# Two and six PSUM banks in place of three and five, in a kernel of two transformer layers

## The chip, the cores and the metric

The kernel runs on one core of one Trainium2 chip. The metric is the device time of one launch in microseconds (us); lower is better. The engines have these names in the profile: PE is TensorE (matmuls), PEld the loading of its weights, DVE is VectorE, ACT is ScalarE, POOL is GpSimd, SP issues most of the transfers (DMA).

## The reference, cut to what matters

Two layers run one after the other on 256 tokens (T) of width 2048, all in fp32. What matters here is that nearly all the work is products of the activations with big weight matrices, with smaller work between them:

```
proj = x @ w_in + b_in                        # layer 1, 42 column tiles of 128 here
y_conv = silu(layer_norm(conv31(c_val * sigmoid(c_glu)))) * silu(c_gate)
y_attn = window_attention_with_sinks(q, k, v) * silu(a_gate)
x = layer_norm(alpha * x + concat(y_conv, y_attn) @ w_out + b_out)
h = rms_norm(x)                               # layer 2
... = split(h @ w_in_2)                       # sparse attention (NSA), gated linear attention (GLA)
x = x + concat(o_nsa, o_gla) @ w_out_2
x = x + cross_attention(rms_norm(x), rms_norm(mem)) @ w_co
x = x + (silu(gg) * uu) @ w_down              # gg, uu = split(rms_norm(x) @ w_gu)
```

## The kernel before

**Products.** A weight matrix is read in pieces of 128 x 1024 fp32 numbers. `fetch` loads a piece into a ring of four buffers (`st`, L309), ACT rounds it to `hi` (L312) and DVE takes the rest `lo = st - hi` (L313); `hi` and `lo` have rings of four too. Three products of hi and lo parts stand for one fp32 product. `fm2` (through `mm2`, L350 and L352) makes one output tile of 128 columns from two pieces: sixteen matmuls of 512 columns with the hi weights (against hi and lo activations side by side) and sixteen of 256 columns with the lo weights, all summed in one PSUM bank. `tm` (with `mm3`, L325 to L327) makes tokens times 512 columns: it fills two banks at once, one for each half of the tokens (`ti`), from eight pieces; for each piece six matmuls go to the first bank and six to the second.

**PSUM.** The eight banks are two pools. `pp` holds what the projections sum, `pa` what all the rest needs: scores, transposes, values and column sums of the side work. A pool hands out its banks in turn as they are released, and a bank may be written again once the last reader of its former tile is done. `tm(..., alt=True)` takes its second bank from `pa`.

**Reading a bank out.** In layer 1 (`block1`) ACT reads the tile's second half with bias (L666) and then DVE adds the first half (L668). The output projections add to x on DVE (L868 and L869, L1383 and L1384), layer 2 and the FFN use ACT and DVE (`both`, L355 and L356). After four of the eight `tm` products `headtm` normalises the heads: ACT squares both banks (L481), DVE reduces (L482), makes a reciprocal root in eleven small steps (L426 to L431) and only then reads each bank for the last time (L489). In `cross` the output projection `wco` makes five tiles at once and then eleven single ones of twelve matmuls each, added to x on DVE (L1493).

**Side work and order.** Convolution taps (30 DVE instructions of a channel tile, L613), attention, GLA, NSA and norms are generators in two queues. Each piece that a projection takes lets them run for a budget (`rate`, 2.4 in `block1`), so they stand between the projections in program order. The framework then lays out each engine's queue before the run: program order is the priority, and an instruction whose input or buffer isn't ready lets later ones pass. At run time each engine takes its queue in order. In `block1` the projections' order is `PROJ1`: value and gate tile of a convolution channel in turn with queries, gates, keys. The first three tiles are made while x arrives, in two `pp` banks and one of `pa` (`native`).

In the rows below, the 39 `fm2` tiles of `block1` are counted 0 to 38; with three `pp` banks tile n takes over the bank of tile n-3.

Of the kernel before, what the change touches and what calls it, by code (L numbers as in the profile page):

```python
# [5 lines left out]
F32 = mybir.dt.float32  # L6
# [7 lines left out]
P = 128  # L14
T = 256
# [174 lines left out]
class Kern:  # L190
# [55 lines left out]
        return self.sl.tile(shape or [P, 16 if tag[0] == "A" else 8, T], dt, name=f"{tag}_{self.cnt}", tag=tag)  # L246

    def pp(self):
        return self.ps.tile([P, 512], F32, name="pp", tag="pp", bufs=3)

    def pa(self):
        return self.ps.tile([P, 512], F32, name="pa", tag="pa", bufs=5)

    def t1(self, shape=(P, T), dt=F32):
        return self.tmp.tile(list(shape), dt, name="t1", tag="t1", bufs=4)
# [1140 lines left out]
    def cross(self):  # L1396
# [54 lines left out]
        def turn(h):  # L1451
            pt = self.pa()
            for m in range(2):
                for ti in range(2):
                    nc.tensor.transpose(pt[:, m * T + ti * P:m * T + (ti + 1) * P],
                                        S[:, h, ti, m * P:(m + 1) * P], self.ident)
            nc.scalar.copy(PT[:, h * 2:h * 2 + 2].rearrange("p m t -> p (m t)"), pt)

        def values(h):
            po = self.pa()[:, :T]  # L1460
            for m in range(2):
                nc.tensor.matmul(po, cv[:, m, h * P:(h + 1) * P], PT[:, h * 2 + m], start=m == 0, stop=m == 1)
            o = self.t1()
            nc.scalar.copy(o, po)
            self.split(oh[:, h], ol[:, h], o)

        st = self.blockstream(self.i["wcq"])
        for h in range(4):
            ps = self.pp()[:, :T]
# [13 lines left out]
        st = self.blockstream(self.i["wco"])  # L1483
        self.h = self.act_slots()
        for grp in CO_GROUPS:
            ps = [(self.pp() if n < 3 else self.pa())[:, :T] for n in range(len(grp))]
            for k in range(4):
                for n in range(len(grp)):
                    self.mm3(ps[n], next(st), acts[k], k == 0, k == 3)
                if grp[0] == 0:  # L1490
                    (lambda: values(2), lambda: turn(3), lambda: values(3), lambda: None)[k]()
            for n, i in enumerate(grp):
                nc.vector.tensor_add(self.x[:, i], ps[n], self.x[:, i])  # L1493
            for i in grp:
                self.gsplit(self.h[i][0], self.h[i][1], self.x[:, i], self.col("g_ffn", i))
# [55 lines left out]
```

## Time and profile before

| | |
|---|---|
| median of 3 runs | 1623.46 us (1622.9 to 1625.03) |
| the profiled execution | 1624.13 us, of which the span of the profile is 1622.1 us |
| busy: PE, PEld, DVE, ACT, POOL | 99%, 86%, 71%, 54%, 1% of the span |
| granted TensorE clock | 1.00 throughout |
| DMA | 300.31 MB, mean 185 GB/s |

Busy time of PE counts modelled ends of pipelined matmuls. A row of the timeline says when the first instruction of a run of equal ones started, how long the run took, the engine, line and operation, `out<-in` by the program's names, and in brackets how long the engine had been idle and whose end released it.

### The profile page before, as it was taken

What the parts mean: (1) busy time and instruction counts of PE and PEld (TensorE: products, weight loads), DVE (VectorE), ACT (ScalarE), POOL (GpSimd) and SP (SyncE); (2) the same over time, 40 slices, a digit from 0 to 9 for tenths busy, and PEclk for the clock granted to TensorE, in tenths of its full rate; (3) what the DMA queues carried; (4) which work ended last, traced back from release to release, by engine and by line L of the source; (5) the groups of instructions that cost most, each with busy time, mean ns of one, the idle gap of its engine ahead of it and who ended that gap; (6) DMA issues with size and microseconds to landing.
All of it is one profiled execution on the core that took longest, in us unless ns stands there. A gap on an engine that the chain in (4) does not pass through costs nothing.

```text
span 1622.1 us, 24991 instructions
## 1 busy us (share of the span) xinstructions
PE 1604.6 (99%) x9400; PEld 1402.9 (86%) x9400; DVE 1147.5 (71%) x2191; ACT 872.7 (54%) x1435; POOL 20.3 (1%) x36
## 2 busy tenths in 40 slices
PE   8999999999999999999999999999999999999999
PEld 7888888888888878888898888888888888888888
DVE  5999998889778746776678666666666666444443
ACT  7466388558755354765447544554554455333332
POOL 0000000000100011000000000000000000000000
PEclk9999999999999999999999999999999999999999
DMA  7455465655655585345554555555555565556663
GB/s 261 165 171 160 141 226 169 219 188 189 210 193 169 184 290 183 104 143 186 191 170 133 190 185 187 194 191 183 193 191 186 188 192 192 195 195 198 198 197 109
DMA packets 84809, 300.31 MB, mean 185 GB/s; under 512 B 9456, under 2 KB 12144, under 8 KB 84304
## 3 DMA queue, kind: packets, MB, share of 16 engines
q1 hardware_dynamic: 81504, 293.01, 55.2%
q0 software_dynamic: 880, 3.61, 0.6%
q10 hardware_dynamic: 2304, 2.10, 0.4%
q8 instruction: 74, 1.21, 0.3%
q14 instruction: 47, 0.39, 0.1%
HBM read 295.53 MB, written 3.15 MB: 184 GB/s over the span
## 4 chain that ended last, share of the span: by engine, by line
PE 83%; DVE 10%; ACT 3%; DMA 2%; issue 1%; SPq 0%; ACTq 0%; DVEq 0%
PE pp L350 42%; PE pp L352 22%; PE pp L325 4%; PE pp L327 4%; PE pp L326 4%; DVE lo L313 3%; DVE hn L613 2%; DVE B L613 2%; DMA st<-in_w 2%; ACT hi L312 1%; PE pa L1231 1%; PE pa L327 1%; PE pa L325 1%; PE pa L326 1%; DMA cols<-in_cols 0%
## 5 line engine op out<-in xcount | busy, mean ns | idle before, releaser
L313 DVE TENSOR_TENSOR lo<-st,hi 128x1024 fp32r<-128x1024 f32 x528 | 633.1, 1220 | 356.6 <-PE pp L352 193.7
L312 ACT CAST hi<-st 128x1024 fp32r<-128x1024 f32 x528 | 553.8, 1050 | 561.1 <-PE pp L350 389.2
L350 PE MATMUL pp<-A,hi 128*128 128x512 f32 x2368 | 571.8, 392 | 1.2 <-DVE B L668 1.2
L350 PEld LDWEIGHTS pp<-A,hi 128*128 128x128 f32 x2368 | 434.2, 188 | 86.2 <-issue 2.3
L352 PEld LDWEIGHTS pp<-A,lo 128*128 128x128 f32 x2368 | 305.0, 191 | 15.1 <-DVE lo L313 2.7
L352 PE MATMUL pp<-A,lo 128*128 128x256 f32 x2368 | 312.1, 283 | 1.7 <-DVE lo L313 1.7
L350 PE MATMUL pp<-C,hi 128*128 128x512 f32 x512 | 123.0, 391 | 0.4 <-DVE C L405 0.3
L350 PEld LDWEIGHTS pp<-C,hi 128*128 128x128 f32 x512 | 94.0, 188 | 19.3 <-DVE C L405 1.2
L350 PE MATMUL pp<-uB,hi 128*128 128x512 f32 x420 | 100.9, 391 | 0.0
L350 PEld LDWEIGHTS pp<-uB,hi 128*128 128x128 f32 x420 | 77.0, 188 | 14.7
L355 ACT COPY t<-pp 128x256 f32<-128x256 f32 x100 | 37.1, 371 | 72.0 <-PE pp L352 72.0
L325 PE MATMUL pp<-hi,A 128*128 128x512 f32 x176 | 70.2, 399 | 0.1
L327 PE MATMUL pp<-hi,A 128*128 128x512 f32 x176 | 69.1, 392 | 0.0
L326 PE MATMUL pp<-lo,A 128*128 128x512 f32 x176 | 68.6, 390 | 0.0
L352 PEld LDWEIGHTS pp<-C,lo 128*128 128x128 f32 x512 | 65.6, 191 | 2.5
L352 PE MATMUL pp<-C,lo 128*128 128x256 f32 x512 | 66.4, 283 | 0.0
L350 PE MATMUL pp<-uC,hi 128*128 128x512 f32 x240 | 57.2, 391 | 0.0
L613 DVE SCALAR_TENSOR_TENSOR B<-B,cols,B 128x256 f32<-128x256 f32 x120 | 57.1, 477 | 0.0
L352 PEld LDWEIGHTS pp<-uB,lo 128*128 128x128 f32 x420 | 54.3, 191 | 2.3
L352 PE MATMUL pp<-uB,lo 128*128 128x256 f32 x420 | 55.1, 283 | 0.0
L613 DVE SCALAR_TENSOR_TENSOR hn<-B,cols,hn 128x256 f32<-128x256 f32 x112 | 53.3, 476 | 0.0
L350 PEld LDWEIGHTS pp<-uC,hi 128*128 128x128 f32 x240 | 44.1, 188 | 8.5
(423 smaller groups left out, 1712.1 us busy)
## 6 DMA issues: line engine op xcount, KB each, us to landing
st<-in_wgu SPq DMA_DIRECT2D x176, 512.0 KB, 4.1
st<-in_wdn SPq DMA_DIRECT2D x88, 512.0 KB, 4.0
st<-in_w SPq DMA_DIRECT2D x78, 512.0 KB, 3.9
st<-in_wo SPq DMA_DIRECT2D x64, 512.0 KB, 4.2
st<-in_w2t SPq DMA_DIRECT2D x48, 512.0 KB, 4.3
st<-in_w2f SPq DMA_DIRECT2D x42, 512.0 KB, 3.5
raw<-in_wc SPq DMA_DIRECT2D x16, 512.0 KB, 5.2
st<-in_wck SPq DMA_DIRECT2D x8, 512.0 KB, 4.3
```

The source lines that it names most:

```text
L312: nc.scalar.copy(hi, st)
L313: nc.vector.tensor_sub(lo, st, hi.bitcast(F32))
L325: nc.tensor.matmul(ps, sh, mh, start=first, stop=False)
L326: nc.tensor.matmul(ps, sh, ml, start=False, stop=False)
L327: nc.tensor.matmul(ps, sl, mh, start=False, stop=last)
L350: nc.tensor.matmul(ps, sh, acts[k][2], start=k == 0, stop=False)
L352: nc.tensor.matmul(ps[:, :T], sl, acts[k][0], start=False, stop=k == n - 1)
L355: self.nc.scalar.copy(out, ps[:, T:])
L613: nc.vector.scalar_tensor_tensor(t, hp[:, k:k + T], self.col("conv_w", w + k), t, op0=OP.mult, op1=OP.add)
L1231: nc.tensor.matmul(o, PT[b][:, s:s + P], kk[:, 4 + j * 2 + b, g * P:(g + 1) * P], start=False, stop=b == 1 and j == ti)
```

## The change

The pool `pp` gets two banks in place of three, `pa` six in place of five. The first group of the `wco` projection, which sums five tiles at once, takes two from `pp` and three from `pa` in place of three and two. All instructions, their sizes and their program order stay.

```
     def pp(self):
-        return self.ps.tile([P, 512], F32, name="pp", tag="pp", bufs=3)
+        return self.ps.tile([P, 512], F32, name="pp", tag="pp", bufs=2)

     def pa(self):
-        return self.ps.tile([P, 512], F32, name="pa", tag="pa", bufs=5)
+        return self.ps.tile([P, 512], F32, name="pa", tag="pa", bufs=6)
@@ cross
         for grp in CO_GROUPS:
-            ps = [(self.pp() if n < 3 else self.pa())[:, :T] for n in range(len(grp))]
+            ps = [(self.pp() if n < 2 else self.pa())[:, :T] for n in range(len(grp))]
```

## Rows read from the trace of the kernel before

**Rows 1.** The page's busy time, share of the span and instructions of each engine.

```profile
PE 1604.6 (99%) x9400; PEld 1402.9 (86%) x9400; DVE 1147.5 (71%) x2191; ACT 872.7 (54%) x1435; POOL 20.3 (1%) x36
```

**Rows 2.** Waits of all engines: total us, times, longest.

```profile
ACT t L355 <- PE pp L352: 72.0, 88, 0.9
```

**Rows 3.** Busy us (and instructions) by stretch: PE, PEld, DVE, ACT, POOL; clock, DMA.

```profile
38.00:70.00 32.00, 29.41 (x168) 25.25 (x167) 31.17 (x71) 15.53 (x25) 0.00 (x0) 1.00 0.41 136
```

**Rows 4.** Timeline of PE: first matmuls of tiles 6, 7, 10, 18 and 26.

```profile
61.58 1.35 PE L350 MATMUL pp<-A,hi 128*128 128x512 f32 x5
...
68.90 1.39 PE L350 MATMUL pp<-A,hi 128*128 128x512 f32 x5 [0.68 <-DVE B L668]
...
89.45 3.92 PE L350 MATMUL pp<-A,hi 128*128 128x512 f32 x16
...
137.81 3.82 PE L350 MATMUL pp<-A,hi 128*128 128x512 f32 x16
...
192.52 3.70 PE L350 MATMUL pp<-A,hi 128*128 128x512 f32 x15
```

**Rows 5.** Timeline of DVE: last reads of tiles 4, 8, 16 and 24.

```profile
68.33 0.42 DVE L668 SCALAR_TENSOR_TENSOR B<-pp,B 128x256 f32<-128x256 f32 x1
...
94.67 0.41 DVE L668 SCALAR_TENSOR_TENSOR B<-pp,B 128x256 f32<-128x256 f32 x1
...
142.50 0.41 DVE L668 SCALAR_TENSOR_TENSOR B<-pp,B 128x256 f32<-128x256 f32 x1
...
197.45 0.41 DVE L668 SCALAR_TENSOR_TENSOR B<-pp,B 128x256 f32<-128x256 f32 x1
```

**Rows 6.** Timeline: last matmuls of tiles 7 and 20, and their last reads.

```profile
76.07 1.11 PE L352 MATMUL pp<-A,lo 128*128 128x256 f32 x8
...
80.14 0.42 DVE L668 SCALAR_TENSOR_TENSOR B<-pp,B 128x256 f32<-128x256 f32 x1
...
159.27 2.08 PE L352 MATMUL pp<-A,lo 128*128 128x256 f32 x16
...
165.95 0.41 DVE L668 SCALAR_TENSOR_TENSOR B<-pp,B 128x256 f32<-128x256 f32 x1
```

**Rows 7.** Timeline: first matmuls of tile 0; ACT's read of the first native tile.

```profile
26.77 3.84 PE L350 MATMUL pp<-A,hi 128*128 128x512 f32 x16
...
28.33 0.47 ACT L666 ACTIVATE t<-pp,cols 128x256 f32<-128x256 f32 x1
```

**Rows 8.** Timeline: first matmul of `wcv`, last read of `wck`'s first bank; DVE's groups between.

```profile
388.87 0.39 PE L325 MATMUL pp<-hi,B 128*128 128x512 f32 x1
...
402.75 0.74 DVE L489 SCALAR_TENSOR_TENSOR hn<-pp,rmtok,nw 128x512 f32<-128x512 f32 x1
...
L313 DVE TENSOR_TENSOR lo<-st,hi 128x1024 fp32r<-128x1024 f32 x5 | 6.1, 1215 | 0.0
```

**Rows 9.** Timeline: the second query product's first matmul; the first one's last read.

```profile
626.49 0.39 PE L325 MATMUL pp<-hi,A 128*128 128x512 f32 x1
...
631.39 0.75 DVE L489 SCALAR_TENSOR_TENSOR hn<-pp,rtok,nw 128x512 f32<-128x512 f32 x1
```

**Rows 10.** Timeline: the second query product's last read; `pa` instructions alone by stretch.

```profile
667.34 0.75 DVE L489 SCALAR_TENSOR_TENSOR hn<-pp,rtok,nw 128x512 f32<-128x512 f32 x1
...
656.93:668.09 11.16, 8.69 (x71) 8.10 (x71) 0.00 (x0) 3.63 (x14) 1.00 0.44 142
```

**Rows 11.** Timeline in `wco`: first matmuls of tiles 10 and 11, last read of tile 8.

```profile
873.33 0.28 PE L325 MATMUL pp<-C,hi 128*128 128x256 f32 x1
...
875.12 0.38 PE L325 MATMUL pp<-C,hi 128*128 128x256 f32 x1 [0.19 <-DVE A L1493]
...
874.65 0.42 DVE L1493 TENSOR_TENSOR A<-pp,A 128x256 f32<-128x256 f32 x1
```

**Rows 12.** PE's idle time before instructions on `pa` tiles: until, us, times; the largest two.

```profile
  DVE t L668: 1.9, 1
  DVE B L668: 1.3, 2
```

## The prediction

> **What bounds the kernel now.** First the page's busy times: PE is busy for 1604.6 of 1622.1 us, so PE sets the end, and all its idle time together, 17.5 us, is the most that any change of order could give back [rows 1]. A new wait of PE is paid in full, unless PE does something in it that it would have had to do later anyway. So the question is which matmuls would find their bank taken.
>
> The second view is the list of waits. In the FFN, the longest stage, ACT waits for PE before it reads a bank (88 waits of at most 0.9 us): reading follows at once and two banks are enough there [rows 2]. The third is the busy time by stretch. Layer 1 is different: from 38 to 70 us DVE is busy for 31.17 of 32 us and PE for 29.41 [rows 3]. DVE is a second bound there, and it takes its queue in program order, so the last read of a tile (L668) stands behind the convolution taps that were put in front of it. The timelines of PE and DVE show the result, tile by tile: tile 4's bank comes free at 68.33 + 0.42 = 68.75, and tile 6 had begun at 61.58. The three banks are used up even so: tile 7 begins at 68.90 after 0.68 us of idling for that very read [rows 4, 5].
>
> **What the change removes, adds and moves.** No instruction comes or goes. Tile n must now wait for the last read of tile n-2, not n-3. PE takes its queue in order, so behind a waiting matmul stand all later matmuls that the layout has put there, and behind those the rings: a piece's `hi` and `lo` are released later, so ACT's and DVE's next splits and SP's next loads are late too. These have cover, since PE, the engine they feed, is late by the same amount.
>
> *Layer 1, the start.* Tile 0 begins at 26.77 on the third bank; now it needs the first native tile's, which ACT frees at 28.33 + 0.47 = 28.80: 2.0 us [rows 7]. This belongs to the first of four crowded stretches and is no extra term, because it moves tile 6 by as much.
>
> *Layer 1, four crowded stretches.* In each I take the tile with the greatest overlap of "bank free" and "begun two tiles on" [rows 4, 5]: 68.75 - 61.58 = 7.17; 95.08 - 89.45 = 5.63; 142.91 - 137.81 = 5.10; 197.86 - 192.52 = 5.34. If DVE kept its own times throughout, PE would move by the greatest of these alone, 7.2 us. If DVE were late by all that PE is late before each stretch, they would add up to 23.2 us. In between lies what DVE can catch up while it is less loaded. Tile 7's last matmul ends at 76.07 + 1.11 = 77.18 and its bank is free at 80.56, 3.38 us later; one ACT read and one DVE read take 0.47 + 0.41 = 0.9, so 2.5 us are catch-up. Tile 20's bank is free 166.36 - 161.35 = 5.0 us after its end: 4.1 us of catch-up [rows 6, 7]. I give the second quiet stretch the first one's 2.5. PE's delay is then 7.2; 7.2 - 2.5 + 5.6 = 10.3; 10.3 - 2.5 + 5.1 = 12.9; 12.9 - 4.1 + 5.3 = 14.1 us. I take 14.1, with 7.2 and 23.2 as ends.
>
> By the Trainium skill (Perfetto Trace Analysis, section Matmuls) independent groups should rotate through different banks, so that one group's reading overlaps the next one's matmuls. Read as "one bank filling, one being read", two would do and this term would be nothing. The FFN's waits agree [rows 2]; the 7.17 us of overlap at tile 6 does not [rows 4, 5].
>
> *`wck` to `wcv`.* `wck` fills both `pp` banks, and `headtm` reads its first bank until 402.75 + 0.74 = 403.49, while `wcv` begins at 388.87 on the third [rows 8]. `wcv`'s second bank is from `pa`, so PE can go ahead with that half: four pieces in the ring, 24 matmuls. A run of sixteen such matmuls lasts 3.82 us [rows 4], or 0.23 each, so 5.5 us, to 394.4. From there it waits. DVE gets to its read sooner: of its five `lo` splits in that stretch [rows 8] four belong to pieces for which the ring has no room while PE waits, at 1.14 us from start to start, a little under their 1215 ns. That makes 403.5 - 4.6 = 398.9 and a wait of 4.5 us. Ends: 0 (if other work is found) and 403.5 - 394.4 = 9.1.
>
> *The two query products.* The second begins at 626.49; both `pp` banks belong to the first, whose first bank is free at 631.39 + 0.75 = 632.14 [rows 9]. In the kernel before the third bank covers this time: PE runs its half ahead. Neither half has a bank now, and the side work that is next needs what `headtm` makes. 5.65 us, all of it; at least 4 if DVE leaves out a split on the way.
>
> *After the second query product.* Its first bank is free at 667.34 + 0.75 = 668.09, and the next `fm2` can't begin at 656.93. Side work covers most: its matmuls take 8.69 of these 11.16 us [rows 10]. I take the rest, 2.5 us; ends 0 and 4.
>
> *`wco`'s single tiles.* Tile 8's bank is free at 875.07, tile 10 began at 873.33: 1.7 us; even three banks wait there, 0.19 us [rows 11]. The later overlaps are part of the same shift. Ends 0 and 3.
>
> *`pa`.* Before matmuls on `pa` PE's longest waits are 1.9 and 1.3 us, and what ends them is the reading of a projection (L668), the data they work on; a sixth bank leaves that as it is [rows 12]. I take 0.
>
> The sum: 14.1 + 4.5 + 5.65 + 2.5 + 1.7 = 28.5 us. The profiled execution took 1624.13, so 1652.6; it lies 0.7 over the median of the runs shown, and against that I say 1652.
>
> **Rivals.**
>
> *A: the waits are filled.* The layout sees a missing bank and lets side work pass, for which there now is a sixth bank. For it: in the first crowded stretch PE already mixes two tiles and attention scores [rows 4]. Against it: side work is little beside the projections in layer 1, and at 626.49 there is none. Within 0.2%: 1623 to 1627. It decides if all of layer 1's waits are covered and the query products' 5.65 is halved.
>
> *B: faster.* The place is attention in layer 1: a sixth bank lets the next scores run while DVE is late with the last ones. The price it could win is the 3.2 us of PE waiting before `pa` matmuls, or up to the 17.5 us of idle time [rows 1, 12]. 1624.1 - 3.2 = 1621, some 1618 at best, from the point where A holds as well. Against it: those waits name projections as what ends them.
>
> *C: part only.* DVE keeps its own times in layer 1 and little is left elsewhere: 1627 to 1634.
>
> *D: more.* The crowded stretches add up (23.2), `wcv` waits 9.1, the other ends hold: 23.2 + 9.1 + 5.65 + 4 + 3 = 45, so 1669, and above if the late rings starve DVE between the stretches: 1671 to 1685.
>
> **How the numbers follow.** Chances: the forecast, 1634 to 1671, 0.70; A 0.09; B 0.06; C 0.07; D 0.08. From 0.2% (3.2 us) on, a measurement of this kernel can tell a change from none. Faster: B, 0.06; within: A, 0.09; slower: the rest, 0.85. The range of 1628 to 1674 holds the forecast's 0.70, nearly all of C and half of D, about 0.8.
>
> **What would show it.** In the changed kernel's profile PE should be busy for about as long (1604 us) in a span some 28 us longer. PE's waits should name DVE L668 with the most (some 14 us before L350 matmuls of layer 1), then L489 with 12 to 13 us before L325 and L350, with a gap of 5 to 6 us on PE between the two query products. From the FFN on both kernels should run at one pace. The prediction is wrong if layer 1 ends less than 5 us or more than 23 us later than before, if PE has no gap between the query products, or if the time lost lies where I have no term. As the largest term rests on how much DVE catches up, it is the likeliest to be off.

## The result, and the profile after

The changed kernel takes 1648.34 us (median of four runs, 1647.57 to 1649.04) against 1623.65 for the kernel before beside it: a ratio of 1.0153, 95% interval 1.0141 to 1.0165, so 24.7 us slower. Forecast were 1652 us with a range of 1628 to 1674, and slower at 0.85. Span for span (1646.8 against 1622.1) it is 24.7 as well; the forecast's terms summed to 28.5.

The page's busy times after, and from the list of PE's waits five rows (what PE was about to do and which end released it; total us, times, longest):

```profile
PE 1608.5 (98%) x9400; PEld 1405.0 (85%) x9400; DVE 1149.6 (70%) x2191; ACT 875.0 (53%) x1434; POOL 20.5 (1%) x36
```

```profile
PE pp L325 <- DVE hn L489: 10.0, 2, 5.6
...
PE pp L350 <- DVE B L668: 4.9, 3, 1.8
PE pp L325 <- DVE A L1493: 2.0, 5, 1.2
...
PE pp L350 <- DVE hn L489: 1.3, 1, 1.3
PE pp L350 <- DVE t L668: 1.1, 1, 1.1
```

The reads named are the forecast ones, but their shares are not: L668 has 4.9 + 1.1 = 6.0 us where "some 14" was forecast, L489 has 10.0 + 1.3 = 11.3 (forecast 12 to 13). PE is busy 3.9 us longer than before [rows 1] though it does the same matmuls. Comparing when the same matmul begins in the two traces says where the time went:

| up to the first matmul of | before | after | later by | added here | forecast |
|---|---|---|---|---|---|
| `wck` (layer 1 is done) | 366.10 | 367.89 | 1.79 | 1.8 | 14.1 |
| the first `fm2` tile behind `wcv` | 411.59 | 422.17 | 10.57 | 8.8 | 4.5 |
| the first query product | 603.66 | 616.12 | 12.45 | 1.9 | 0 |
| the second `fm2` tile behind the query products | 673.13 | 694.94 | 21.81 | 9.4 | 5.65 + 2.5 |
| the FFN (`wco` is done) | 882.41 | 907.05 | 24.64 | 2.8 | 1.7 |
| the end of the span | 1622.1 | 1646.8 | 24.7 | 0.1 | 0 |

**Layer 1.** PE's timeline: first matmuls of tiles 5 and 6, the last ones of tile 6, first ones of tiles 7 and 18, which answer to [rows 4]:

```profile
60.78 3.94 PE L350 MATMUL pp<-A,hi 128*128 128x512 f32 x16 [1.33 <-DVE B L668]
...
69.24 3.93 PE L350 MATMUL pp<-A,hi 128*128 128x512 f32 x16 [1.76 <-DVE B L668]
73.01 2.08 PE L352 MATMUL pp<-A,lo 128*128 128x256 f32 x16
74.92 1.32 PE L350 MATMUL pp<-A,hi 128*128 128x512 f32 x5
...
141.41 0.96 PE L350 MATMUL pp<-A,hi 128*128 128x512 f32 x3 [1.77 <-DVE B L668]
```

DVE's last reads of tiles 4, 8, 16 and 24, which answer to [rows 5]:

```profile
68.77 0.42 DVE L668 SCALAR_TENSOR_TENSOR B<-pp,B 128x256 f32<-128x256 f32 x1
...
93.12 0.42 DVE L668 SCALAR_TENSOR_TENSOR B<-pp,B 128x256 f32<-128x256 f32 x1
...
140.94 0.42 DVE L668 SCALAR_TENSOR_TENSOR B<-pp,B 128x256 f32<-128x256 f32 x1
...
195.63 0.42 DVE L668 SCALAR_TENSOR_TENSOR B<-pp,B 128x256 f32<-128x256 f32 x1
```

Tile 6 does begin 7.66 us later, at the very moment at which tile 4's bank comes free (69.19), as forecast. But DVE's reads are not late along with PE: the four come 0.44 us later and 1.55, 1.56 and 1.82 us earlier than before. And a tile's late beginning is not work that is late: before, PE put five of its matmuls in at 61.58 [rows 4], went back to tile 5's lo half and only then on with tile 6, as the next rows of that timeline show. Tile 6 ends at 75.08 against 72.59, 2.5 us later, not 7.7.

```profile
62.78 1.11 PE L352 MATMUL pp<-A,lo 128*128 128x256 f32 x8
63.73 2.69 PE L350 MATMUL pp<-A,hi 128*128 128x512 f32 x11
```

What the layer loses by this is small. Busy time from 28 to 276 us, asked for in three stretches, of which the line of sums is shown (us, then busy us of each engine), first after, then before:

```profile
sum 248.00, PE 238.92 PEld 207.93 DVE 239.58 ACT 161.60 POOL 0.00; mean PE 79.64 PEld 69.31 DVE 79.86 ACT 53.87 POOL 0.00
```

```profile
sum 248.00, PE 241.59 PEld 209.03 DVE 240.08 ACT 162.68 POOL 0.00; mean PE 80.53 PEld 69.68 DVE 80.03 ACT 54.23 POOL 0.00
```

DVE is busy for 240.08 of the 248 us before and for 239.58 after, so it loses 0.5 us; PE's idle time grows from 6.4 to 9.1 us. What PE gives up is lead over the reading. Its last matmuls of tile 24, before and after, which go with that tile's reads at 197.45 [rows 5] and 195.63:

```profile
181.53 2.07 PE L352 MATMUL pp<-A,lo 128*128 128x256 f32 x16
```

```profile
184.57 2.07 PE L352 MATMUL pp<-A,lo 128*128 128x256 f32 x16
```

The tile ends 3.0 us later and is read 1.8 us earlier. Over the 39 tiles the time from a tile's last matmul to the end of its last read is 7.2 us on average before and 4.0 us after. PE's tiles end 1.3 to 5.3 us later, but this does not add up from stretch to stretch: the last tile ends 2.2 us later, and `wck` begins 1.8 us later (first row before, second after).

```profile
366.10 0.48 PE L325 MATMUL pp<-hi,B 128*128 128x512 f32 x1
```

```profile
367.89 0.48 PE L325 MATMUL pp<-hi,B 128*128 128x512 f32 x1
```

**`wck` to `wcv`.** PE's timeline, and DVE's three instructions that matter in it, which answer to [rows 8]:

```profile
395.71 0.49 PE L325 MATMUL pa<-hi,B 128*128 128x512 f32 x1 [0.63 <-ACT hi L312]
397.14 0.50 PE L326 MATMUL pa<-lo,B 128*128 128x512 f32 x1 [0.94 <-DVE lo L313]
...
402.95 0.80 PE L325 MATMUL pp<-hi,B 128*128 128x512 f32 x1 [4.38 <-DVE hn L489]
403.55 0.63 PE L326 MATMUL pp<-lo,B 128*128 128x512 f32 x1
...
406.94 0.39 PE L325 MATMUL pp<-hi,B 128*128 128x512 f32 x1
```

```profile
394.69 1.27 DVE L482 TENSOR_REDUCE hss<-t 128x4 f32<-128x512 f32 x2
...
397.01 0.16 DVE L426 TENSOR_SCALAR nw<-hss 128x8 f32<-128x8 f32 x1
...
402.15 1.40 DVE L489 SCALAR_TENSOR_TENSOR hn<-pp,rmtok,nw 128x512 f32<-128x512 f32 x2
```

PE does its 24 matmuls on the `pa` half, with short waits for splits among them, and then stands for 4.38 us until `headtm`'s first read ends at 402.9. Between L426 and L489 DVE takes 5.1 us for eleven small steps of 0.15 us, as other work stands between them in its queue. Then something that the forecast had no term for: the nine matmuls from 402.95 to 406.94 stand 3.99 us / 9 = 0.44 apart, in place of 0.23. The busy times by stretch (after the five engines: granted clock, DMA's share, GB/s) name it, here and behind the gap in front of the second query product:

```profile
403.00:407.00 4.00, 4.00 (x10) 3.15 (x11) 3.38 (x8) 2.63 (x6) 0.00 (x0) 0.51 0.02 4
407.00:411.00 4.00, 4.00 (x23) 3.34 (x22) 3.69 (x7) 4.00 (x9) 0.00 (x0) 1.00 0.15 29
...
645.00:649.00 4.00, 4.00 (x10) 3.13 (x11) 0.37 (x1) 0.00 (x0) 0.00 (x0) 0.50 0.05 17
```

The granted clock is 0.51 and 0.50, the lower of TensorE's two levels (1.2 in place of 2.4 GHz). That explains why PE is busy for 3.9 us longer with the same work: 3.99 - 9 x 0.227 = 1.95 us here, and 2.1 behind the second query product, where ten distances take 4.40 us (4.40 - 10 x 0.227).

**The query products and `wco`.** PE's timeline, which answers to [rows 9 to 11]:

```profile
644.86 0.76 PE L325 MATMUL pp<-hi,A 128*128 128x512 f32 x1 [5.63 <-DVE hn L489]
...
687.33 0.96 PE L350 MATMUL pp<-A,hi 128*128 128x512 f32 x3 [1.26 <-DVE hn L489]
...
891.93 0.39 PE L325 MATMUL pp<-C,hi 128*128 128x256 f32 x1 [1.25 <-DVE A L1493]
893.79 0.39 PE L325 MATMUL pp<-C,hi 128*128 128x256 f32 x1 [0.16 <-DVE A L1493]
```

The gap between the query products was forecast at 5.65 and is 5.63. From the FFN on the delay stays at 24.6 to 24.7 us for over 700 us: two banks are enough there, as [rows 2] said.

### The profile page after: what moved, and what is told of

Read it like the earlier page. It is cut to its first block, busy times and chain, and to the rows that moved or that the text cites. A ratio compares the mean times of both kernels' runs of the same rounds, so it can differ in the third digit from the quotient of the medians.

```text
span 1646.8 us, 24875 instructions
## 1 busy us (share of the span) xinstructions
PE 1608.5 (98%) x9400; PEld 1405.0 (85%) x9400; DVE 1149.6 (70%) x2191; ACT 875.0 (53%) x1434; POOL 20.5 (1%) x36
## 4 chain that ended last, share of the span: by engine, by line
PE 86%; DVE 9%; ACT 2%; DMA 1%; issue 1%; SPq 0%; ACTq 0%; DVEq 0%
PE pp L350 46%; PE pp L352 24%; PE pp L325 3%; PE pp L326 3%; PE pp L327 3%; DVE lo L313 2%; DVE hn L613 1%; DVE B L613 1%; DMA st<-in_w 1%; ACT hi L312 1%; DVE A L409 1%; PE pa L1231 1%; DMA cols<-in_cols 0%; PE pa L1186 0%; PE pa L325 0%
```

## The experiments

The theory after the traces: the loss is the missing third `pp` bank in three places, `wcv`, the second query product and `wco`, with the clock's fall as a part of the first two; layer 1 pays little because DVE keeps its own times. Rivals: the forecast's sizes (layer 1 the largest term); other waits take the place of those removed; the sixth `pa` bank hides part of the loss. Medians and ratios are against runs of the kernel before on the same chip (1623.4 to 1623.9 us).

**`wcv` on two banks of `pa`; the second query product on two of `pa`; both.**

```
-        ps = [self.pp(), self.pa() if alt else self.pp()]
+        ps = [self.pa() if alt == 2 else self.pp(), self.pa() if alt else self.pp()]
-        psv = self.tm(self.i["wcv"], 0, macts, alt=True)
+        psv = self.tm(self.i["wcv"], 0, macts, alt=2)        # first and third
-            psv = self.tm(w2t, 4 + c, acts)
+            psv = self.tm(w2t, 4 + c, acts, alt=2 * c)       # second and third
```

> The changed kernel, but `wcv` takes both its banks from `pa`. My theory: the 8.8 us that are lost between `wck` and `wcv` (gaps of PE of 0.8, 1.2 and 4.55 us, and the matmuls after the long gap at a granted clock of 0.51) are all the missing bank's, and nothing else moves: 1648.3 - 8.8 = 1639.5 us, 1638.5 to 1640.5, with no gap of PE over 1 us before `wcv` and a clock of 1.0 from 396 to 411. Rival: DVE's splits set the pace there, so another wait takes the gap's place: 1646 to 1649.

> The changed kernel, but the second query product takes both its banks from `pa`. My theory: this takes away the 5.8 us gap between the two query products, the matmuls at half the granted clock behind it (some 2 us) and the later `fm2` wait of 1.3 us for L489, in all the 9.35 us by which this stretch fell behind: 1648.3 - 9.35 = 1639.0 us, 1638 to 1640.5. Rival: only the gap goes and something of the stretch's loss stays, since `headtm`'s reads still come late: 1642 to 1644 us.

> The changed kernel with both edits, `wcv` and the second query product each on two banks of `pa`. My theory: the two losses lie in separate stages with no cover in common, so they add: 1648.3 - 8.8 - 9.35 = 1630.2 us, 1629 to 1632. What is left, 6.7 us over the kernel before, is layer 1 (1.8), small ones (2.0) and `wco` (2.9). Rival: what one gives back the next stage takes again: 1635 to 1640 us.

Measured: 1641.58 us (ratio 1.0111, 1.0096 to 1.0126), 1639.09 (1.0094, 1.0079 to 1.0109) and 1629.63 (1.0038, 1.0023 to 1.0052). With both, 18.7 us come back of 24.7 (expected 18.15). The first gave 6.8 by its runs, 2 us less than expected and 1.1 past the expected range, though the two intervals are wide enough for 8.8. In its trace the stretch from `wck` to the `fm2` tile behind `wcv` lost 0.13 us in place of 8.78, so the cause is shown; whether the 2 us are chance or are lost elsewhere stays open. The second gave 9.25 (expected 9.35); in its trace the stretch from the first query product to the second `fm2` tile behind, which had lost 9.36 us, gains 0.7 on the kernel before. With both edits no other long wait takes their place. Busy time by stretch with both edits, over the same stretch of `wcv`:

```profile
396.00:403.00 7.00, 7.00 (x33) 5.79 (x32) 7.00 (x20) 6.95 (x15) 0.00 (x0) 1.00 0.57 193
403.00:407.00 4.00, 4.00 (x23) 3.14 (x22) 4.00 (x7) 2.40 (x5) 0.00 (x0) 1.00 0.83 289
```

PE is busy throughout at a clock of 1.00, 23 matmuls in the four us that held 10 in the changed kernel. DVE is as loaded as in the kernel before (busy for all of these 11 us there too): it did not get faster, PE only had another bank.

**Two and five: one bank left unused.**

```
-        return self.ps.tile([P, 512], F32, name="pa", tag="pa", bufs=6)
+        return self.ps.tile([P, 512], F32, name="pa", tag="pa", bufs=5)
```

> The changed kernel with `pa` at five banks again, `pp` at two, so that one PSUM bank is left unused. My theory: the sixth bank of `pa` is worth nothing here, all the difference is the third bank of `pp`: 1648.3 us as the changed kernel, 1647 to 1650. Rival: the sixth bank hides part of the loss (side work passes a waiting projection): 2 to 8 us more, 1650 to 1656.

Measured: 1648.72 us (1.0155, 1.0140 to 1.0170), as the changed kernel. The sixth bank of `pa` is worth nothing here that the runs can tell; the forecast's 0 for `pa` was right, and rivals A and B, which needed it, had no ground.

**Two `pp` banks in layer 1 alone, and three in layer 1 alone.** Layer 1 here is `block1`, without its output projection. The third bank is a pool of its own that every third tile takes; `pa` has five, and in the first kernel `wco`'s group of five is as before; `s` is the stage about to run.

```
     def pp(self):
-        return self.ps.tile([P, 512], F32, name="pp", tag="pp", bufs=2)
+        self.turn = (getattr(self, "turn", -1) + 1) % 3
+        px = self.turn == 2 and not self.layer1      # other kernel: and self.layer1
+        return self.ps.tile([P, 512], F32, name="pp", tag="px" if px else "pp", bufs=1 if px else 2)
...
-                s()
+                self.layer1 = s == self.block1; s()
```

> The change in layer 1 alone: `pp` has two banks in `block1` and three elsewhere, `pa` five, `wco` as before. My theory after the traces: DVE kept its own times in layer 1, so two banks cost what the changed kernel was late at the start of `wck`, 1.8 us: 1623.5 + 1.8 = 1625.3 us, 1624.3 to 1627, with `wck` beginning 1 to 2.5 us later than in the kernel before. Rival, the prediction's step: the crowded stretches add up to 14.1 us: 1637.6, 1633 to 1641.

> The complement: three `pp` banks in `block1`, two from there on, `pa` five. My theory: the whole loss but layer 1's 1.8 us stays, 1648.3 - 1.8 = 1646.5 us, 1645 to 1648. Rival, the prediction's sizes: without its layer 1 term of 14.1 the change would cost 14.4 us, 1623.5 + 14.4 = 1637.9, 1635 to 1641.

Measured: 1626.32 us (1.0017, 1.0008 to 1.0026), so 1.3 to 4.2 us for layer 1 with two banks, and the forecast's 14.1 is ruled out. In its trace `wck` begins 0.40 us later than before, short of the 1 to 2.5 expected:

```profile
366.50 0.48 PE L325 MATMUL pp<-hi,B 128*128 128x512 f32 x1
```

Over the eight traces with two `pp` banks in `block1` (the changed kernel and seven of the experiments) it is -0.01 to 3.12, mean 1.2, and much of the spread is there at the first tile (-0.40 to 1.67). In all eight the mean time from a tile's end to its last read is 3.9 to 4.0 us; in the three traces with three banks it is 7.2.

The other one: 1648.27 us (1.0149, 1.0135 to 1.0163). Of the expected 1.8 us nothing shows in the median, 0.3 us past the expected range, though the two intervals are too wide to exclude 1.8. Its trace shows why the terms need not add up: `wck` does begin 1.75 us earlier than in the changed kernel, and `wcv` begins 1.75 us earlier after the same wait, but behind it the low clock lasts longer.

```profile
401.20 0.80 PE L325 MATMUL pp<-hi,B 128*128 128x512 f32 x1 [4.38 <-DVE hn L489]
...
406.49 0.98 PE L497 MATMUL pa<-misc,hn 128*128 128x128 f32 x4
407.20 0.51 PE L325 MATMUL pp<-hi,B 128*128 128x512 f32 x1
```

It is 0.50 from 401.20 to 407.0 and 0.87 in the microsecond behind, against 402.95 to 406.9 in the changed kernel: 1.0 us of the 1.75 is lost in this one stretch. All but 0.1 of the rest is gone by the first query product.

**PE kept busy in the two gaps.** Added matmuls on data that is there, into a `pa` bank that nothing reads: extra work that leaves the output as it is.

```
+    def warm(self, n, w, mv):
+        ps = self.pa()
+        for _ in range(n):
+            self.tc.keep_in_program_order(self.nc.tensor.matmul(ps[:, :mv.shape[-1]], w, mv, start=True, stop=True))
...
+        self.warm(40, macts[0][0][:, :P], macts[0][0])            # ahead of wcv
+            c and self.warm(20, acts[0][0][:, :P], acts[0][2])    # ahead of the second query product
```

> The changed kernel with added matmuls on data that is there, written to a `pa` bank that nothing reads: 40 of 256 columns ahead of `wcv` and 20 of 512 columns ahead of the second query product, so that PE is busy in most of its two long waits (4.55 and 5.8 us). My theory: the matmuls behind these waits ran at granted clocks of 0.51 and 0.50 because PE had stood idle; with PE busy the clock stays near 1.0 there and about 2 us come back at each place: 1648.3 - 4 = 1644.3 us, 1643 to 1646, with matmul distances of 0.23 in place of 0.43 us right behind the waits. Rival: the low clock comes from the stage or the matmuls themselves, not from the idling: 1648 us or more, as the added matmuls take their own time, 1647.5 to 1651.

Measured: 1646.97 us (1.0141, 1.0124 to 1.0158): short of the 1643 to 1646 expected, and by the runs the interval reaches over the changed kernel's 1.0153, so the total alone doesn't settle it. The trace does, on the clock. PE's timeline at the two places, and two stretches right behind the waits:

```profile
391.99 4.96 PE L1539 MATMUL pa<-B 128*128 128x256 f32 x40
...
404.28 0.50 PE L325 MATMUL pp<-hi,B 128*128 128x512 f32 x1 [1.87 <-DVE hn L489]
...
640.11 4.70 PE L1539 MATMUL pa<-A 128*128 128x512 f32 x20
645.91 0.47 PE L325 MATMUL pp<-hi,A 128*128 128x512 f32 x1 [1.11 <-DVE hn L489]
```

```profile
404.00:408.00 4.00, 3.72 (x18) 3.13 (x19) 3.58 (x8) 2.47 (x6) 0.00 (x0) 1.00 0.00 0
...
645.00:649.00 4.00, 3.09 (x15) 2.57 (x16) 1.41 (x2) 0.06 (x1) 0.00 (x0) 1.00 0.25 98
```

The same projection matmuls run at 1.00 where they had run at 0.51 and 0.50. The first nine distances behind `wcv`'s wait take 2.18 us in place of 3.99, the first ten behind the other 2.37 in place of 4.40: 1.8 and 2.0 us come back, as expected. That the whole gained only about 1.4 has two visible causes: this execution's layer 1 ended 1.3 us later than the changed kernel's, and the second query product's bank came free 1.1 us later. So it is the idling, not the stage, that brings the clock down.

**Three and four; four and four.**

```
-        return self.ps.tile([P, 512], F32, name="pp", tag="pp", bufs=2)
+        return self.ps.tile([P, 512], F32, name="pp", tag="pp", bufs=3)    # other kernel: 4
-        return self.ps.tile([P, 512], F32, name="pa", tag="pa", bufs=6)
+        return self.ps.tile([P, 512], F32, name="pa", tag="pa", bufs=4)
```

> The kernel before with one bank of `pa` left unused: `pp` three, `pa` four. My theory: the side work needs no more than four at once, or hardly: 1623.5 us as the kernel before, 1622 to 1626; then the bank to give away lies in `pa`, not in `pp`. Rival: `pa` is as tight as `pp`: 5 to 20 us slower, 1628 to 1644.

> The opposite change: four banks of `pp` and four of `pa`. My theory: three `pp` banks already leave PE only about 1.5 us of waits for them, and four `pa` banks cost 3 us (the run with three and four), so nothing is won: 1623.4 + 3.0 - 1 = 1625.4 us, 1623.5 to 1627. Rival: DVE's crowded stretch in layer 1 profits from a fourth bank by more than `pa` loses: 1619 to 1622 us, faster than both kernels.

Measured: 1626.46 us with three and four (1.0016, 1.0007 to 1.0026), 3.0 slower, half a microsecond past the expected end; its loss lies elsewhere than that of the change, 1.55 of it in `cross`. The fifth bank of `pa` is worth an eighth of the third one of `pp`. With four and four 1624.22 (0.9999, 0.9990 to 1.0008): no difference, and no gain from a fourth bank. Its trace is the clearest sign that early tiles in layer 1 are not progress: tile 18 begins at 133.26, 4.5 us earlier than before, and `wck` only 0.2 earlier. Three of PE's largest waits in the whole trace, and the sum from 28 to 276 us:

```profile
PE pp L350 <- ACT hi L312: 2.0, 2, 1.7
PE pp L325 <- ACT C L404: 1.3, 2, 0.9
PE pp L352 <- DVE lo L313: 1.3, 3, 0.6
```

```profile
sum 248.00, PE 243.25 PEld 208.40 DVE 238.41 ACT 160.33 POOL 0.00; mean PE 81.08 PEld 69.47 DVE 79.47 ACT 53.44 POOL 0.00
```

L668 is gone from in front of `pp` matmuls, and PE waits for the splits of the pieces instead. The mean time from a tile's end to its last read is 7.9 us with four banks, against 7.2 with three and 4.0 with two: more banks let PE run further ahead and leave the layer's end nearly where it was. That DVE's work sets that end is the likely reason, argued from its load; no run here changed that work.

**All spread: both edits above, and more of `wco` on `pa`.** By the condition in the edit every third single tile (6, 9, 12 and 15) takes its bank from `pa`, and so does the whole first group of five, whose first tile is number 0; the expectation names the single tiles alone.

```
-            ps = [(self.pp() if n < 2 else self.pa())[:, :T] for n in range(len(grp))]
+            ps = [(self.pp() if n < 2 and grp[0] % 3 else self.pa())[:, :T] for n in range(len(grp))]
```

> Two and six banks, with `wcv` and the second query product on two banks of `pa` each, and every third single tile of `wco` on one of `pa`. My theory: `wco`'s 2.85 us go too, as tile n then again waits for one of three banks: 1629.6 - 2.9 = 1626.7 us, 1625.5 to 1628.5, still 2 to 4 us over the kernel before. Rival: `wco`'s loss lies in DVE's own pace at L1493, so the bank doesn't matter: 1629.6, 1628.5 to 1631.

Measured: 1627.15 us (1.0017, 1.0008 to 1.0026), 2.5 us below the run with both edits; in `wco` its trace gains 0.86 us on the kernel before where the other lost 2.84. About 0.9 of these 3.7 us lie in the first twenty of the 64 steps of three matmuls, before the waits for L1493 had begun, so they come from elsewhere, most likely from the first group's banks; the rest goes with those waits, which are gone. So of the 24.7 us 21.2 are undone without a third `pp` bank, and that `wco` waits for a bank is shown as well. Neither this nor any other version run beats the kernel before.

## Why the prediction was right in its sum and wrong in its largest term

Slower was right, and by about how much was luck: a term that was 12.3 us too large and others that were 8.5 us too small nearly cancelled. The forecast named its own test: it "is wrong if layer 1 ends less than 5 us" later than before. It ended 1.8 us later.

- **The step that failed: layer 1, the four crowded stretches, 14.1 us.** The forecast took the overlap of "bank free" and "begun two tiles on" as PE's loss, and let DVE be late along with PE. Both halves are wrong. A tile that begins early is one that PE has a few matmuls of, among other tiles' (tile 6: begins 7.66 us later, ends 2.5 later). And DVE was hardly late: busy for 97% of the layer, it had other work (taps, splits) to do, and made the four reads of [rows 5] at -1.8 to +0.4 us of their old times. What the third bank had given was lead of PE over the reading, 7.2 us on average in place of 4.0; without it the layer ended 1.8 us later. The forecast read the time from a tile's end to its last read at two quiet tiles only (3.38 and 5.0 us) and took it as a catch-up of DVE. Even the end where "DVE kept its own times", 7.2 us, was four times too high. The layer cost 1.8 us here, 1.3 to 4.2 alone.
- **`wck` to `wcv`, 4.5 us: the right place, mis-sized; 8.8 measured.** Of the term's five splits four should have been left out on the way to L489. DVE did three of them from `wcv`'s start (390.67) to its read, so it left out two, 2.3 us; PE lost 6.8 us from where its 24 matmuls would have ended (390.67 + 5.5) to 402.95. The clock adds 1.95: 6.8 + 1.95 = 8.75. It lies within the ends given (0 to 9.1), but the upper end had no room for the clock.
- **Query products: the gap was right** (5.65 forecast, 5.63 measured), and the wait behind the second one is 1.3 where 2.5 was taken. Left out were the 2.1 us at the low clock. Together they make 9.0 of the 9.4 measured, in place of 8.15; 0.3 is not accounted for.
- **`wco`: the place was right, 2.8 us in place of 1.7.** Its ends were 0 to 3. The forecast took all later overlaps as part of the first shift; in the trace PE waits for L1493 at five tiles, 2.0 us in all.
- **No term at all: 1.9 us between `wcv` and the first query product.** 1.8 of it lies ahead of the sixth `tm` product, in all kernels run with two `pp` banks behind layer 1, and at most 0.3 in those with three or four; a 1.1 us wait of side work (L1088) for ACT stands there. What it comes from was not tried and stays open.
- **`pa`, 0 us, and the FFN at one pace:** right (two and five ran as two and six; 0.1 us over the FFN).

The rule that independent groups should rotate through banks (the Trainium skill, Perfetto Trace Analysis, section Matmuls), read as "two will do", would forecast no loss in any stage. The FFN's 0.1 us agrees with that reading; `wcv` and the query products, where the reader is a chain on DVE, differ from it by 8.8 and 9.4 us.

## What to carry to other kernels

How many banks a loop needs is not told by how far its tiles overlap. A tile's early beginning is lead, and lead is worth only what it later covers: compare when tiles end and when their reader takes them, and ask whether the reader would be late too. Here an overlap of 7 us cost 1.8 us, since DVE, nearly full with other work, read at nearly its old times. The price of a bank lies where a single long chain (here a head norm of a reduce, eleven small steps and a last read) holds all banks of a pool and nothing else is queued for PE. Such a product can get its banks from the other pool, which bought back 18.7 of 24.7 us. And in this kernel PE's waits of 4.38 and 5.63 us cost some 2 us more than their length: look at the granted clock behind a long wait and add what it takes.

## What the runs showed of the hardware that was not expected

The granted TensorE clock, 1.00 throughout before, fell to half behind PE's idling of 4.38 us (after two short waits of 0.63 and 0.94) and of 5.63 us: 0.51 and 0.50 for about 4 us each, and for 5.8 us in the kernel with three banks in layer 1, behind the same 4.38 us. In the changed kernel it cost some 2 us each time, on top of the wait. Behind the single waits of 1.3 to 1.8 us in layer 1 (tiles 5, 6 and 18 above) it stayed at 1.00. Filling the gaps with matmuls that nobody needs kept it at 1.00. The Trainium skill (TensorE: Matmul & The Clock Gate, section HAM oscillation — how this bites in real kernels) tells of a kernel where waits for DMA did this before every batch; here waits for a PSUM bank do, and the two stretches at 0.51 and 0.50 agree with it.
